# Retention's value product ahead of attention's output product, in a two-layer hybrid decoder

## The chip, the cores and the metric

The kernel runs on one core of one Trainium2 chip, in one launch. The time is the device time of one execution in microseconds (us), the median of several runs. TensorE (PE) does matrix products, VectorE (DVE) and ScalarE (ACT) do elementwise work, GpSimd (POOL) and SyncE (SP) issue DMAs here. Each engine takes its own instructions strictly in order and waits on semaphores for the others.

## The reference

There are 512 tokens of 1024 features, two layers, everything in fp32. One layer is:

```
h  = rmsnorm(x, g_mix)
aq, ak, av, rq, rk, rv, rg, ga, gb = split(h @ w_in)       # one projection
ya = sliding_window_attention(rope(aq), rope(ak), av, sinks) @ w_a
r  = retention(rot(rq), rot(rk), rv)                       # 4 heads, causal, decayed
yb = (groupnorm(r) * silu(rg)) @ w_b
x  = x + (sigmoid(ga) * ya + sigmoid(gb) * yb) @ w_out
x  = x + square(relu(rmsnorm(x, g_mlp) @ w_up)) @ w_down
```

A final rmsnorm gives the output. Attention has 8 query heads of 64 over 2 key heads, in blocks of 128 queries against a band of 256 keys, with one learned sink logit per head.

## The kernel before

**Products.** Activations lie feature by token in SBUF. Every fp32 operand is split into a high part (rounded to fp32r, by ACT: `hi`, L334) and a rest (by DVE: `lo`, L335), and one fp32 product is three PE matmuls, high x high, low x high, high x low (L386 to L388). A *unit* is 128 x 1024 of weights: 512 KB, loaded by SP into one of five buffers `raw`, split into one of four `hi` and four `lo`, used by 24 matmuls. `unit_order` writes down the order of all units once. Loads run four units ahead of splits, splits three units ahead of products. `chunk` takes one unit of `w_in` and makes 128 output features of all tokens. Units of the projection (38 in a layer) come as: a group of four (key, value, two query chunks), two query chunks, eight chunks of `ga`, rk and rq of head 0, rg 0 to 3, rk and rq of heads 1, 2, 3, rg 4 to 7, eight chunks of `gb`.

**Block products.** Retention's values `rv` (512 x 1024) and the MLP's matrices are multiplied by a scheme with seven half-size products in place of eight. `values` is that product for `rv`: 14 units (seven parts of two). It needs sums of quarters of the weights and of the activations. The sums of activations are made by `Turned`: four copies `xg` of 512 KB each are read back from DRAM (from the input `xT` in layer 0, from `spill` in layer 1), scaled by ACT (L882), added and subtracted by DVE (L885 to L888) and split (L406, L407). `load(0)` and `load(2)` issue two copies each, `build(0)` and `build(2)` do the arithmetic. The copies lie in a pool `big` of six buffers (4 KB in each partition) that they share with attention's result `whole`, with the tables and with the retention gates `z`, so a copy waits until its buffer is given back.

**Weight-sum jobs.** The sums of weights are made in DRAM: `sum_steps` is a list of jobs, each a DMA on POOL that copies a quarter (0.5 or 1 MB) and one that adds another onto it. `pace(src)` is called after the evacuation of a chunk; on every second call POOL copies one column of `src` (`mark`, which makes it wait for that evacuation) and then issues the next job.

**Attention** runs as a background generator. Its queries are rotated, split, and, for two layouts, partly copied between partitions by 16 DMAs of 64 KB on SP (`beside`, L658: `r<-qlo`); four more do the same for the keys. Then come 16 steps (4 blocks of 128 queries x 4 pairs of heads): scores on PE (`score`, L771), softmax on DVE and ACT, transposes (`pT`, L736), and per block the weighted values (`pv`, L756 and L757), whose sum `whole` is split into `a_h`, `a_l`. `advance(rate)` takes steps of it between the halves of a chunk.

**The stretch between attention and retention.** After the last step of attention stand two units (rk and rq of head 1) with `build(0)` behind them, then the four units of `w_a` (attention's output product on `a_h`, `a_l`), with `build(2)` in their middle, then `values`, at the end of which the generator `retention(0)` starts (heads 0 and 1), then rk and rq of heads 2 and 3, then rg 4 and 5.

**Clean-ups.** ACT writes some PSUM banks, and PE then adds onto them. Such a bank first gets a matmul that clears its accumulation flags: `ones` x `xh`. `values` has one for its bank of the pool `ps_aux`; in the MLP `wash` issues one or two after the first block's `w_up` chunks.

**Order.** Engines get their instructions from a scheduler that orders the program with its own estimate of times when it is built. It moves work of later program text ahead where it expects an engine to be free. The order is then fixed.

Of the kernel before, what the change touches and what calls it, by code (L numbers as in the profile page):

```python
# [17 lines left out]
P = 128  # L18
T = 512
# [31 lines left out]
DELAY = 2  # L51
AHEAD = 4
SPLIT = 3


def unit_order(layer):

    order = [("w_in", i) for i in range(4 + 2 + 8 + 2 + 4 + 2)]
    order += [("w_a", i) for i in range(4)]
    order += [("rv", part, u) for part in range(7) for u in range(2)]  # L60
    order += [("w_in", i) for i in range(22, 34)]
    order += [("w_b", i) for i in range(4)]
# [12 lines left out]
    return order  # L75
# [39 lines left out]
def decoder(ctx, tc, xT, x_first, w_in, w_rv, w_a, w_b, w_out, w_up, w_pair, w_down, w_end, tables, decay, band, g_last, out):  # L115
    nc = tc.nc
# [493 lines left out]
    def layer_body(layer):  # L610
# [48 lines left out]

        def put_k(ps):  # L660
            r = rotate(ps, attn_tabs, layer == 0)
            pace(r)
            lo = big("klo")[:, 0, :]
            for g in range(N_KV):
                nc.scalar.activation(kh[g], r, AF.Copy)
            nc.vector.tensor_tensor(lo, r, f32(kh[0]), ALU.subtract)
            for g in range(N_KV):
                nc.vector.tensor_scalar(kl[g], lo, half[:, g : g + 1], None, ALU.mult)
                beside(g, kh[g], kh[g])
# [23 lines left out]
        def put_q(c):  # L693
            def put(ps):
                r = rotate(ps, attn_tabs, layer == 0 and c < 2)
                pace(r)
                if c % 2 == 0:
                    qlo[:] = [big("qlo")]
                lo = qlo[0][:, c % 2, :]
                for g in range(N_KV):  # L700
                    nc.scalar.activation(q_s[g][:, c, :], r, AF.Copy)
                nc.vector.tensor_tensor(lo, r, f32(q_s[0][:, c, :]), ALU.subtract)
                for g in range(N_KV):
                    beside(g, q_s[g][:, c, :], lo)

            return put
# [205 lines left out]
        def values(turned, while_last):  # L912
# [7 lines left out]
            def multiply(ps, moving, start=True, meanwhile=None):  # L920
                for u in range(2):
                    hi, lo = unit("rv", layer)
                    if meanwhile:
                        meanwhile()
# [41 lines left out]
            put(0, 1, c, 1, two)  # L966
            multiply(b, turned[3], False)
            put(1, 1, b, -1, five)
            while_last()
            multiply(b, turned[4], False, advance)  # L970
            turned.free(1)
            put(1, 0, b, -1)

# [98 lines left out]
        def retention(pair):  # L1072
            two = [Head(2 * pair), Head(2 * pair + 1)]
            for head in two:
                for js in ((0, 1), (2, 3)):
                    head.scores(js)
                    if pair == 0 and head is two[1] and js[0]:
                        load_decay(1)
# [12 lines left out]
            yield  # L1091
            yield
            two[1].norm()
            yield
# [19 lines left out]
        qk(1)  # L1114
        turned.build(0)
        turned.load(2)


        aT = [(a_h[:, c, :], a_l[:, c, :]) for c in range(4)]
        for u in range(4):  # L1120
            hi, lo = unit("w_a", layer)
            for j in range(2):
                c = 2 * u + j
                ps = bank(ps_mm, "mm")
                pairs = []
                for k in range(4):
                    cols = slice(k * 256 + j * P, k * 256 + (j + 1) * P)
                    pairs.append(((hi[:, cols], lo[:, cols]), aT[k]))
                products(ps, pairs, True, True)
                nc.vector.tensor_tensor(mixed[c], mixed[c], ps, ALU.mult)  # L1130
            if u == 1:
                turned.build(2)
                load_decay(0)
        for t in a_t:
            slots.give(*t[1])

        values(turned, lambda: background.append(retention(0)))
        qk(2, 1.2)
        qk(3, 1.2)
        for i in (4, 5):  # L1140
            chunk("w_in", layer, xs, put_rg(i), 1.2)
        drain()
        background.append(retention(1))
        for i in (6, 7):
# [239 lines left out]
        def down(e, into):  # L1384
# [16 lines left out]
            a, c = ([bank(ps_mm, "mm") for _ in range(2)] for _ in range(2))  # L1401
            b = [bank(ps_aux, "b") for _ in range(2)]
            multiply(a, b11)
            for m in range(2):
                nc.scalar.activation(b[m], a[m], AF.Copy)
            multiply(c, u_forms[0])
# [166 lines left out]
        def first_hooks():  # L1573
# [11 lines left out]
                    nc.scalar.activation(sq[:, 0:1], factor[:, 0:1], AF.Sqrt)  # L1585
                sum_input(2)

            def wash():
                for ps in used:
                    nc.tensor.matmul(ps, ones, xh[:, 0, :], start=True, stop=True)  # L1590

            return at0, at1, wash

        for e in range(N_BLOCK):
            if e == 0:
                into = Adding(e)
                hooks = first_hooks()
                for c in (0, 2):
                    two_chunks("w_up", layer, xs, [put_up(c), put_up(c + 1)], hooks[c // 2])
                hooks[2]()  # L1600
# [51 lines left out]
def _w_in_units(w):  # L1652
# [11 lines left out]
    def qk(h):  # L1664
        return _units_chunks(w, pairs(O_RK, h)) + _units_chunks(w, pairs(O_RQ, h))
# [4 lines left out]
    units += qk(0)  # L1670
    units += _units_chunks(w, O_RG + r(T))
    units += qk(1)
    units += qk(2) + qk(3)
    units += _units_chunks(w, O_RG + T + r(T))
    units += _units_chunks(w, O_GB + r(D))
    return units

# [108 lines left out]
```

## Time and profile before

| | us |
|---|---|
| three runs | 1508.51, 1501.99, 1509.72 (median 1508.51) |
| the profiled execution | 1502.61, of which its span is 1500.8 |
| PE busy | 1465.7, 98% of the span |
| DVE busy | 1124.4, 75% |
| ACT busy | 949.0, 63% |
| POOL busy | 218.1, 15% |
| granted PE clock, mean | 0.99 of full speed |

PE is busy all but 35 us of the span. In the views below a wait is put down to what ended it; a time stands in us from the start of the span, layer 0 takes the first half and layer 1 the second.

### The profile page before, as it was taken

To read this page: it belongs to the slowest core of one execution; us is meant where nothing else is said; L and a number is where in the kernel's file an instruction comes from. 1 tells how busy PE (TensorE), PEld (TensorE's weight loads), DVE (VectorE), ACT (ScalarE), POOL (GpSimd) and SP (SyncE) were. 2 spreads that over 40 slices of the span, in tenths; PEclk is the share of its full clock that TensorE was granted. 3 is DMA by queue.
4 is the path that set the end of the run, shared out by engine and by line. 5 is a ranking of instruction groups with operands and counts; after the bars stand their busy time and mean duration, and the time that the engine had idled before them with its cause. 6 is when DMAs were issued, how large, how long until landed. Compare 5 with 4: busy or idle time off the path is not lost.

```text
span 1500.8 us, 21396 instructions
## 1 busy us (share of the span) xinstructions
PE 1465.7 (98%) x7753; PEld 1262.4 (84%) x7753; DVE 1124.4 (75%) x1697; ACT 949.0 (63%) x1553; POOL 218.1 (15%) x294
## 2 busy tenths in 40 slices
PE   9899999999999999999999988999999999999998
PEld 7688788888889999998877876888888889999997
DVE  6668887865577888888876687787846768888885
ACT  7546656543467777777754475565434767777775
POOL 0210000302211111112202010002120021111120
PEclk9999999999999999999999998999999999999999
DMA  7954653859875777666959646447696286776664
GB/s 256 268 174 137 200 176 105 230 135 282 234 185 189 190 197 182 181 177 196 299 166 293 198 116 188 159 127 196 180 292 187 77 214 187 197 195 173 177 187 154
DMA packets 95867, 287.32 MB, mean 191 GB/s; under 512 B 11152, under 2 KB 11280, under 8 KB 90896
## 3 DMA queue, kind: packets, MB, share of 16 engines
q1 hardware_dynamic: 62544, 175.56, 34.1%
q0 software_dynamic: 32496, 109.07, 32.8%
q8 instruction: 61, 1.00, 0.3%
q10 hardware_dynamic: 720, 1.31, 0.2%
q14 instruction: 46, 0.38, 0.1%
HBM read 246.05 MB, written 107.48 MB: 236 GB/s over the span
## 4 chain that ended last, share of the span: by engine, by line
PE 91%; DMA 4%; DVE 2%; ACT 2%; issue 1%; SPq 0%; ACTq 0%; DVEq 0%
PE mm L386 24%; PE mm L387 24%; PE mm L388 24%; PE b L386 3%; PE b L387 3%; PE b L388 3%; DMA r<-qlo 2%; PE rv L386 2%; PE rv L388 2%; PE rv L387 2%; PE mm L401 1%; DMA xg<-spill 1%; PE score L771 1%; DVE lo L335 1%; PE r L388 1%; PE r L387 1%
## 5 line engine op out<-in xcount | busy, mean ns | idle before, releaser
L334 ACT ACTIVATE hi<-raw 128x1024 fp32r<-128x1024 f32 (+1 forms) x375 | 382.4, 1020 | 319.3 <-PE mm L387 190.0
L335 DVE TENSOR_TENSOR lo<-raw,hi 128x1024 fp32r<-128x1024 f32 (+1 forms) x376 | 438.8, 1173 | 145.5 <-ACT hi L334 143.6
L386 PE MATMUL mm<-xh,hi 128*128 128x512 f32 (+1 forms) x976 | 345.4, 356 | 1.8 <-DVE z L983 1.0
L387 PE MATMUL mm<-xl,hi 128*128 128x512 f32 (+1 forms) x976 | 344.1, 355 | 0.0
L388 PE MATMUL mm<-xh,lo 128*128 128x512 f32 (+1 forms) x976 | 342.6, 356 | 0.0
L386 PE MATMUL mm<-r,hi 128*128 128x256 f32 (+1 forms) x736 | 239.7, 329 | 8.1 <-ACT r L406 7.6
L387 PE MATMUL mm<-r,hi 128*128 128x256 f32 (+1 forms) x736 | 240.0, 326 | 0.0
L388 PE MATMUL mm<-r,lo 128*128 128x256 f32 (+1 forms) x736 | 240.0, 326 | 0.0
L386 PEld LDWEIGHTS mm<-xh,hi 128*128 128x128 f32 x976 | 185.4, 190 | 26.7 <-ACT xh L409 1.2
L387 PEld LDWEIGHTS mm<-xl,hi 128*128 128x128 f32 x976 | 185.5, 190 | 24.5
L388 PEld LDWEIGHTS mm<-xh,lo 128*128 128x128 f32 x976 | 184.6, 190 | 24.6
L386 PEld LDWEIGHTS mm<-r,hi 128*128 128x128 f32 x736 | 141.3, 192 | 22.4 <-ACT r L406 8.4
L387 PEld LDWEIGHTS mm<-r,hi 128*128 128x128 f32 x736 | 140.6, 191 | 13.3
L388 PEld LDWEIGHTS mm<-r,lo 128*128 128x128 f32 x736 | 140.5, 191 | 11.8 <-DVE lo L335 0.2
L1464 POOL DMA_DIRECT2D y<-eu x56 | 62.2, 1341 | 370.6 <-DVE eu L1449 370.6
L387 PE MATMUL mm<-lo,r 128*128 128x512 f32 (+1 forms) x276 | 104.5, 388 | 0.0
L388 PE MATMUL mm<-hi,r 128*128 128x512 f32 (+1 forms) x276 | 101.4, 387 | 0.0
L386 PE MATMUL mm<-hi,r 128*128 128x512 f32 (+1 forms) x276 | 98.5, 390 | 0.4 <-ACT r L406 0.2
L386 PE MATMUL b<-hi,r 128*128 128x512 f32 x180 | 70.5, 392 | 0.0
L387 PE MATMUL b<-lo,r 128*128 128x512 f32 x180 | 70.3, 391 | 0.0
L388 PE MATMUL b<-hi,r 128*128 128x512 f32 x180 | 67.8, 390 | 0.0
L270 DVE TENSOR_TENSOR raw<-raw 128x512 f32<-128x512 f32 x56 | 38.6, 690 | 36.5 <-DMA raw<-w_pair_in 25.4
(300 smaller groups left out, 2410.6 us busy)
## 6 DMA issues: line engine op xcount, KB each, us to landing
raw<-w_in_in SPq DMA_DIRECT2D x73, 512.0 KB, 4.4
sums_down<-w_down_in POOLq DMA_DIRECT2D x30, 1024.0 KB, 10.5
sums_up<-w_pair_in POOLq DMA_DIRECT2D x56, 512.0 KB, 8.9
raw<-w_down_in SPq DMA_DIRECT2D x45, 512.0 KB, 7.2
raw<-w_pair_in SPq DMA_DIRECT2D x84, 256.0 KB, 3.8
y<-y POOLq DMA_DIRECT2D x64, 256.0 KB, 9.2
y<-eu POOLq DMA_DIRECT2D x62, 256.0 KB, 8.1
raw<-sums_down SPq DMA_DIRECT2D x30, 512.0 KB, 7.5
```

The costliest lines, as they stand in the source:

```text
L270: nc.vector.tensor_tensor(raws[i][:, at], last[:, LEFT], last[:, RIGHT], ALU.add)
L334: nc.scalar.activation(hi[:, at], raw[:, at], AF.Copy)
L335: nc.vector.tensor_tensor(lo[:, at], raw[:, at], f32(hi[:, at]), ALU.subtract)
L386: nc.tensor.matmul(ps, ah, bh, start=start and i == 0, stop=False, **more)
L387: nc.tensor.matmul(ps, ah, bl, start=False, stop=False, **more)
L388: latest[0] = nc.tensor.matmul(ps, al, bh, start=False, stop=stop and i == n - 1, **more).ins
L401: latest[0] = nc.tensor.matmul(ps, w[:, cols(j, c)], moving[k][low], start=first, stop=bool(final)).ins
L771: nc.tensor.matmul(ps[:, g * w : (g + 1) * w], q_s[g][:, c, at], part[:, keys], start=i == 0, stop=i == 1)
L1464: nc.gpsimd.dma_start(y[:, 2 * j + m, i * T : (i + 1) * T], t, **how)
```

## The change

The stretch between attention and retention is reordered. After rk and rq of head 1 now stand rg 4 and rg 5, then `values`, then the units of `w_a`; `retention(0)` starts after `w_a`, and rk and rq of heads 2 and 3 advance it at a rate of 2.0 in place of 1.2. `build(2)` and the first decay table come ahead of `values`. The host lays the weights out in the new order. `pace` is no longer called at the key and the queries (5 calls fewer in a layer), and is called at the eight chunks of `w_a`. `wash` is gone; the first blocks of the MLP clean the banks that ACT is about to write, right after the product that fills their source. The second decay table is loaded later. The line numbers of the new kernel are higher by one in its first half and lower by one to four from there on.

```diff
+CLEANED = ({1: (0,)}, {0: (0, 1), 1: (0,)})
 def unit_order(layer):
-    order = [("w_in", i) for i in range(4 + 2 + 8 + 2 + 4 + 2)]
+    order = [("w_in", i) for i in range(4 + 2 + 8 + 2 + 4 + 2 + 2)]
+    order += [("rv", part, u) for part in range(7) for u in range(2)]
     order += [("w_a", i) for i in range(4)]
-    order += [("rv", part, u) for part in range(7) for u in range(2)]
-    order += [("w_in", i) for i in range(22, 34)]
+    order += [("w_in", i) for i in range(24, 34)]
@@ put_k @@
             r = rotate(ps, attn_tabs, layer == 0)
-            pace(r)
@@ put_q @@
                 r = rotate(ps, attn_tabs, layer == 0 and c < 2)
-                pace(r)
...
         qk(1)
         turned.build(0)
         turned.load(2)
+        for i in (4, 5):
+            chunk("w_in", layer, xs, put_rg(i))
+        turned.build(2)
+        load_decay(0)
+        values(turned)
@@ the units of w_a @@
                 nc.vector.tensor_tensor(mixed[c], mixed[c], ps, ALU.mult)
-            if u == 1:
-                turned.build(2)
-                load_decay(0)
+                pace(mixed[c])
...
-        values(turned, lambda: background.append(retention(0)))
-        qk(2, 1.2)
-        qk(3, 1.2)
-        for i in (4, 5):
-            chunk("w_in", layer, xs, put_rg(i), 1.2)
+        background.append(retention(0))
+        qk(2, 2.0)
+        qk(3, 2.0)
         drain()
@@ down @@
             multiply(a, b11)
+            with tc.issue_after(latest[0]):
+                for m in CLEANED[last].get(e, ()):
+                    nc.tensor.matmul(b[m], ones, xh[:, 0, :], start=True, stop=True)
...
-            def wash():
-                for ps in used:
-                    nc.tensor.matmul(ps, ones, xh[:, 0, :], start=True, stop=True)
```

PE in layer 0, where the fourth score of attention stands (`score_639` before, `score_631` after; `mm_772` and `mm_764` are the same chunk of `ga`, `pT` a transpose of attention). Before:

```order
L386 MATMUL mm_772<-xh_76,hi_568 128x512
L387 MATMUL mm_772<-xl_77,hi_568 128x512
L771 MATMUL score_639<-r2_83,r0_81 128x128 x2
L771 MATMUL score_639<-r2_83,r1_82 128x128 x2
L736 MATMUL pT_656<-ident_130,sm_537 128x128 x2
L388 MATMUL mm_772<-xh_76,lo_569 128x512
L386 MATMUL mm_867<-xh_76,hi_634 128x512
```

After:

```order
L389 MATMUL mm_684<-xh_76,lo_509 128x512
L387 MATMUL mm_764<-xh_76,hi_557 128x512
L388 MATMUL mm_764<-xl_77,hi_557 128x512
L770 MATMUL score_631<-r2_83,r0_81 128x128 x2
L770 MATMUL score_631<-r2_83,r1_82 128x128 x2
L735 MATMUL pT_648<-ident_130,sm_530 128x128 x2
L389 MATMUL mm_764<-xh_76,lo_558 128x512
```

The score stood one matmul ahead of the end of that chunk and stands now two behind its start: 263 matmuls of chunks are ahead of it before, 242 after.

ACT in layer 0 at the end of attention (`whole` is attention's last result and `r4` its split `a_h`; `rot2` belongs to rk and rq; `xg` are the copies of `Turned`, `t2` the first sum that DVE makes from the first two). Before:

```order
L627 ACTIVATE rot2_1501<-mm_1475 64x512
L628 ACTIVATE rot2_1501<-mm_1475 64x512
L882 ACTIVATE xg_1465<-xg_1465,x_75 128x512 x2
L406 ACTIVATE r4_85<-whole_1372 128x4x128
L627 ACTIVATE rot2_1545<-mm_1519 64x512
L628 ACTIVATE rot2_1545<-mm_1519 64x512
L882 ACTIVATE xg_1466<-xg_1466,x_75 128x512 x2
```

After:

```order
L407 ACTIVATE r4_85<-whole_1364 128x4x128
L881 ACTIVATE xg_1457<-xg_1457,x_75 128x512 x2
L881 ACTIVATE xg_1458<-xg_1458,x_75 128x512 x2
L628 ACTIVATE rot2_1533<-mm_1507 64x512
L629 ACTIVATE rot2_1533<-mm_1507 64x512
L335 ACTIVATE hi_1598<-raw_1461 128x1024
L407 ACTIVATE r2_83<-rot_1492 128x512
L881 ACTIVATE xg_1560<-xg_1560,x_75 128x512 x2
L407 ACTIVATE r0_81<-t2_1549 128x512
```

The split of attention's last result stood behind the first copy's scaling and stands now ahead of it; the third copy's scaling (`xg_1560`) stands now ahead of the first split that `values` reads (`r0<-t2`).

PE in layer 0 at the start of what follows attention (`rv` are the banks of `values`, `ret` scores of retention, `mm_1578` the first bank of `w_a`). Before:

```order
L757 MATMUL pv_1380<-r7_88,r3_84 128x512
L916 MATMUL rv_1726<-xh_76,ones_115 128x512
L386 MATMUL ret_1978<-late_89 128x512
L387 MATMUL ret_1978<-late_89 128x512
L388 MATMUL ret_1978<-late_89 128x512
L386 MATMUL ret_1986<-late_89 128x384
L387 MATMUL ret_1986<-late_89 128x384
L388 MATMUL ret_1986<-late_89 128x384
L386 MATMUL mm_1578<-r4_85,hi_1421 128x512
```

After:

```order
L389 MATMUL rv_1653<-hi_1564,xl_77 128x512
L387 MATMUL ret_2102<-late_89 128x512
L388 MATMUL ret_2102<-late_89 128x512
L389 MATMUL ret_2102<-late_89 128x512
L387 MATMUL ret_2110<-late_89 128x384
L388 MATMUL ret_2110<-late_89 128x384
L389 MATMUL ret_2110<-late_89 128x384
L387 MATMUL rv_1656<-hi_1682,r0_81 128x512
```

Before, the last `pv` of attention is followed by the clean-up, six matmuls of retention and then `w_a`, which reads `a_h`. After, between that last `pv` and the first matmul that reads a sum of `Turned` (`r0`) stand 9 matmuls of rq, 48 of rg 4 and 5, the clean-up, 24 of the first part of `values` and the same six of retention in layer 0; in layer 1, where the last `pv` stands in the middle of rg 4, it is 9 of rg 4, the clean-up, 24 of rg 5, 24 of `values` and the six.

More of the change, by code (lines that the diff above doesn't have):

```diff
@@ L910, in quarter, with values @@
             return [(xh[:, k, at], xl[:, k, at]) for k in range(4 * half, 4 * half + 4)]
-        def values(turned, while_last):
+        def values(turned):
             a, c = ([bank(ps_mm, "rv") for _ in range(2)] for _ in range(2))
@@ L918, in values, with multiply @@
             nc.vector.tensor_scalar(minus, plus, -1.0, None, ALU.mult)
-            def multiply(ps, moving, start=True, meanwhile=None):
+            def multiply(ps, moving, start=True):
                 for u in range(2):
                     hi, lo = unit("rv", layer)
-                    if meanwhile:
-                        meanwhile()
                     for m in range(2):
@@ L968, in values @@
             put(1, 1, b, -1, five)
-            while_last()
-            multiply(b, turned[4], False, advance)
+            multiply(b, turned[4], False)
             turned.free(1)
@@ L1076, in retention @@
                     head.scores(js)
-                    if pair == 0 and head is two[1] and js[0]:
-                        load_decay(1)
                     yield
@@ L1093, in retention @@
             two[1].norm()
+            if pair == 0:
+                load_decay(1)
             yield
@@ L1586, in at1 @@
                 sum_input(2)
-            def wash():
-                for ps in used:
-                    nc.tensor.matmul(ps, ones, xh[:, 0, :], start=True, stop=True)
-            return at0, at1, wash
+            return at0, at1
         for e in range(N_BLOCK):
@@ L1672, in _w_in_units @@
     units += qk(1)
+    units += _units_chunks(w, O_RG + T + r(2 * P))
     units += qk(2) + qk(3)
-    units += _units_chunks(w, O_RG + T + r(T))
+    units += _units_chunks(w, O_RG + T + 2 * P + r(2 * P))
     units += _units_chunks(w, O_GB + r(D))
```

1 line of the change is left out of this document (removed).

## The prediction

> **What bounds the kernel now.** I read the page first, then the waits of PE, the instructions of PE in order of time around each long wait, and last SP, ACT and the copies there.
>
> ```profile
> span 1500.8 us, 21396 instructions
> PE 1465.7 (98%) x7753; PEld 1262.4 (84%) x7753; DVE 1124.4 (75%) x1697; ACT 949.0 (63%) x1553; POOL 218.1 (15%) x294
> ```
>
> PE is the bound: 35.1 us of the span are idle. The change takes no matmul of the reference away, so it can win idle PE time and time at a low clock, nothing else. The waits of PE (total us, times, longest):
>
> ```profile
> PE mm L386 <- ACT r L406: 7.8, 3, 6.3
> PE score L771 <- DMA r<-qlo: 7.4, 5, 5.1
> PE ret L386 <- DVE whole L759: 3.9, 2, 1.9
> PE score L771 <- DVE sm L798: 1.8, 1, 1.8
> PE pT L736 <- DVE st L789: 1.1, 1, 1.1
> PE pv L756 <- ACT r L406: 1.0, 1, 1.0
> PE mm L386 <- DVE z L983: 1.0, 1, 1.0
> PE score L771 <- DVE r L407: 0.4, 1, 0.4
> PE score L771 <- DVE st L779: 0.3, 1, 0.3
> ```
>
> Nearly all of them lie between the queries and `w_a`. In order of time:
>
> ```profile
> 75.26 0.66 PE L771 MATMUL score<-r,r 128*128 128x128 f32 x2 [5.14 <-DMA r<-qlo]
> 163.51 2.08 PE L386 MATMUL mm<-r,hi 128*128 128x512 f32 x4 [1.30 <-ACT r L406]
> 806.22 0.41 PE L771 MATMUL score<-r,r 128*128 128x128 f32 x2 [0.75 <-DMA r<-qlo]
> 908.22 2.07 PE L386 MATMUL mm<-r,hi 128*128 128x512 f32 x4 [6.30 <-ACT r L406]
> ```
>
> After a wait PE's clock (PEclk, third column from the right) is low for some 4 us:
>
> ```profile
> 75.30:79.30 4.00, 3.67 (x12) 3.03 (x13) 2.08 (x6) 1.15 (x5) 0.62 (x1) 0.51 0.69 280
> 163.50:168.00 4.50, 4.49 (x11) 3.53 (x12) 4.43 (x9) 3.62 (x6) 1.33 (x3) 0.50 1.01 189
> 809.00:813.00 4.00, 4.00 (x12) 3.24 (x13) 0.00 (x0) 0.00 (x0) 0.00 (x0) 0.59 1.01 313
> 869.00:877.00 8.00, 5.15 (x32) 3.81 (x31) 7.67 (x26) 7.13 (x20) 0.00 (x0) 1.00 0.22 66
> 908.20:912.20 4.00, 3.98 (x10) 3.17 (x11) 3.79 (x7) 3.02 (x5) 0.00 (x0) 0.51 1.02 240
> 350.00:375.00 25.00, 25.00 (x111) 20.58 (x110) 10.07 (x12) 6.67 (x9) 5.08 (x7) 1.00 1.02 303
> ```
>
> So a cluster of waits costs its idle time and then busy time x (1 - PEclk): 1.8 us at 75, 2.2 at 163, 1.6 at 809, 2.0 at 908, nothing at 869. The last row gives the pitch of matmuls at full clock: 25 / 111 = 0.225 us.
>
> **The change part by part.** *Query copies (weight-sum jobs gone from keys and queries).* Layer 0 waits for `r<-qlo` 7.4 - 0.75 = 6.65 us, and 1.8 follow in low clock: 8.4. Layer 1: 0.75 + 1.82 + 1.6 = 4.2. The copies are slow because jobs fill the queues; the window 40 to 80 us holds
>
> ```profile
> q0 software_dynamic: 1008, 6.82, 62.4%
> q1 hardware_dynamic: 1824, 4.46, 30.4%
> DMA to landing us min/median/max: 6.1/11.1/14.2
> L702 DVE TENSOR_TENSOR qlo<-rot,r x4: 682/685/689, 44.7 to 53.2; 128x512 f32<-128x512 f32 x4
> 51.45 0.69 DVE L832 TENSOR_TENSOR x<-mm,rstd 128x512 f32<-128x512 f32 x1
> 59.65 3.75 SPq L658 DMA_DIRECT2D r<-qlo  x4
> raw<-w_in_in SPq DMA_DIRECT2D x73, 512.0 KB, 4.4
> ```
>
> (q0 carries POOL's jobs; the landing row is that of `qlo`'s copies; the last row is the page's.) The last query is split at 53.2 + 0.7 = 53.9, yet its four copies go out only from 59.65: SP waits for earlier copies. The new order moves its score forward by 263 - 242 = 21 matmuls, 4.7 us: PE was there at 75.26 - 5.14 = 70.1, now at 70.1 - 4.7 - 1.15 (two shorter waits gone) = 64.2. Without jobs I let the four leave 53.9 to 56.4 and land within 4.4 (what 512 KB take at the median) to 6.1 (the fastest copy here): 60.8 to 62.5, in time. One job does remain: the first now hangs on the second chunk of `ga`, evacuated at 51.45. I keep 1.0 us for it in layer 0 and 0.8 in layer 1: **-7.4 and -3.4**. Ends: -8.4 and -4.2, or the rival below.
>
> By the Trainium skill's page "DMA: Bandwidth & Descriptors" (Queues, rings and completion order) each DMA engine takes turns between the queues by packets, so an emptied POOL queue could at best halve the 11.1 us, and a copy still stands behind SP's own weight loads. If the last copy then left at 62.9 as now, it would land at 68.5, the wait be 4.3 and the sum 1490. No run here shows SP's queue alone.
>
> *End of attention.* Waits of 0.97 (layer 0) and 1.09 + 0.97 + 0.45 + 0.32 = 2.83 (layer 1) end on small steps of DVE and ACT. Attention starts earlier and, in layer 1, its last products lie beside rg 4. Gain between 0 and 3.8; I take half: **-1.9**.
>
> *`w_a` moved back.* It waited for the split of `whole`, which ACT held behind a copy's scaling. Gone with it: 1.93 + 1.30 + 2.2 = 5.5 in layer 0 and 1.93 + 6.30 + 2.0 = 10.2 in layer 1. What is late next is the sums themselves: `values` reads them, and `w_a` (96 matmuls, 21.6 us) no longer covers their copies. The third copy waits for `whole`'s buffer, the fourth for the first copy's:
>
> ```profile
> 157.73 0.39 PE L757 MATMUL pv<-r,r 128*128 128x512 f32 x1
> 164.22 0.33 SPq L872 DMA_DIRECT2D xg<-xT_in  x1
> 171.19 1.34 ACT L882 ACTIVATE xg<-xg,x 128x512 f32<-128x512 f32 x2 [1.96 <-DMA xg<-xT_in]
> 173.90 1.04 ACT L334 ACTIVATE hi<-raw 128x1024 fp32r<-128x1024 f32 x1
> 179.39 1.34 ACT L882 ACTIVATE xg<-xg,x 128x512 f32<-128x512 f32 x2 [4.45 <-DMA xg<-xT_in]
> 182.69 0.63 ACT L406 ACTIVATE r<-t 128x512 fp32r<-128x512 f32 x1 [1.01 <-DVE t L886]
> 908.92 0.32 SPq L872 DMA_DIRECT2D xg<-spill  x1
> 916.22 1.34 ACT L882 ACTIVATE xg<-xg,x 128x512 f32<-128x512 f32 x2 [2.14 <-DMA xg<-spill]
> ```
>
> From the last `pv` to the third copy's issue: 6.5 us, of which the scaling in front (1.3) goes and a `hi` split (1.04) comes: 6.2. From that issue to the split of the fourth copy's first sum: 183.3 - 164.2 = 19.1. ACT's new order puts a `hi` and an `r` split, then two `hi` and two 0.6 us sigmoids into it (5 us, of which 1.3 covers DVE's sums): 22.7. Ready at 28.9 after the last `pv`. Layer 0 has in front of it 9 + 48 + 1 + 24 matmuls, retention's six (1.4), and 26 on the first two copies: 108 x 0.225 + 1.4 + 0.2 = 26.0. Wait: 2.9. In layer 1 only 58 matmuls (14.7 us) stand before the first sum, whose split lies behind the third copy's scaling: 6.2 + 7.3 + 1.3 + 1.04 + 3 x 0.6 = 17.7, wait 3.0. Then rg 4's bank, which `values` wants 12 matmuls later (at 20.4), is evacuated only into the second copy's buffer: 17.7 + 0.6 + 1.04 + 0.6 + 1.04 + 1.2 + 0.7 = 22.9, wait 2.5. The fourth copy is hidden there by 1.5. Each layer also pays 1.9 of low clock: new cost 4.8 and 7.4. Net **-0.7 and -2.8**. Ends: no new wait at all, or both copies slow (rivals).
>
> By "TensorE: Matmul & The Clock Gate" (The HAM clock gate) of the Trainium skill the clock falls only after about 3.4 us of idling; then these short waits would cost no clock and the sum be 1482.8. The row at 809 disagrees: waits of 0.75 and 1.82 us were enough.
>
> *The rest.* Retention at rate 2.0 puts its DVE work (some 22 us) beside four chunks in place of six. DVE was full there already while PE never waited:
>
> ```profile
> 1000.00:1025.00 25.00, 25.00 (x114) 20.81 (x113) 25.00 (x34) 14.40 (x22) 4.64 (x6) 1.00 0.69 174
> 1203.22 0.50 PE L1590 MATMUL ssq<-xh,ones 128*128 128x512 f32 x1 [0.25 <-ACT y L1241]
> ```
>
> I cost it at nothing; without that cover it would be some 5 us a layer. The eight new `pace` calls send four jobs (on POOL) beside `w_a`, whose loads on SP are four units ahead; the row at 350 shows DMA queues full (1.02) with PE unbroken. Clean-ups: one matmul more, +0.2, less a wait of 0.25, plus whatever queueing them costs: **+0.2**.
>
> Sum: -7.4 - 3.4 - 1.9 - 0.7 - 2.8 + 0.2 = -16.0. The profiled execution took 1502.61: **1486.6 us**. It is near the fastest of the three runs; from the median (1508.51) the same steps lead to 1492.5. A measurement tells about 0.5% from no change: 1495.1 and 1510.1 on this scale.
>
> **The rivals.** *The sums' copies in series (slower).* The first copies of layer 1 took far longer than the later ones, with jobs around them (landing rows of the copies, 150 to 175 us and 885 to 912 us):
>
> ```profile
> DMA to landing us min/median/max: 4.8/5.5/6.9
> DMA to landing us min/median/max: 7.2/13.1/15.5
> ```
>
> In the new order copies three and four run beside loads of `rv` units and jobs. At 13.1 each, layer 0 loses 5.9 + 7.5 more, layer 1 5.8 + 8.3 - 1.5: 26.0, in all 1512.6. It eats the gain from about 11 us a copy. Against it: 5.5 to 7.3 us for these two in both layers.
>
> *Copies of queries as late as now (no change).* If they still land at 75.2, PE waits there with 21 matmuls fewer done: +4.7 for -7.4, and 0 for -3.4 in layer 1: 1502.1. For it: the first job still goes out ahead of the last copies.
>
> *All new waits covered.* If the copies land a few us earlier and ACT keeps up: -16.0 - 4.8 - 7.4, 1474.4.
>
> **How the numbers follow.** Forecast 0.58 (own range 1478 to 1497), slow copies 0.13, late queries 0.12, all covered 0.17. The range 1473 to 1503 leaves out the slow copies. Faster: 0.54 of the forecast and all covered, 0.71; within 0.5%: 0.04 + 0.12 = 0.16; slower: 0.13.
>
> **What would show it.** Right: no PE wait on `r<-qlo` over 1 us, no `mm` of `w_a` waiting for ACT, new waits of `rv` matmuls on ACT's `r` or DVE, 2 to 6 us a layer, and a wait of ACT on `xg` ahead of them. Wrong: `rv` waits above 8 us a layer, a PE wait on `score` above 4 us, or PE waiting for `lo` splits in the chunks after `w_a`.

## The result, and the profile after

| | median us | runs | ratio to before | 95% interval |
|---|---|---|---|---|
| before | 1505.90 | 1501.99 to 1509.72 (7) | 1 | |
| after | 1494.09 | 1490.09 to 1499.14 (7) | 0.9925 | 0.9900 to 0.9949 |

The change makes the kernel 0.75% faster: 1494.1 us, inside the forecast range, 7.5 us above the forecast. The profiled execution of after took 1498.12 us, one of its longer ones, 4.5 us less than that of before.

From the page of after, its span and busy times:

```profile
span 1496.4 us, 21384 instructions
PE 1464.2 (98%) x7754; PEld 1260.4 (84%) x7754; DVE 1125.0 (75%) x1697; ACT 943.1 (63%) x1549; POOL 217.4 (15%) x294
```

PE is idle for 32.2 us, 2.9 less than before. The waits of PE (total us, times, longest; those at the start, at the end and in the MLP are left out, all but one):

```profile
PE rv L387 <- ACT hi L335: 6.3, 2, 4.8
PE rv L387 <- ACT r L407: 5.9, 2, 4.5
PE rv L387 <- ACT rv L954: 5.7, 1, 5.7
PE rv L389 <- DVE r L408: 1.2, 1, 1.2
PE mm L387 <- DVE z L979: 1.0, 1, 1.0
PE rv L388 <- DVE lo L336: 0.5, 1, 0.5
PE b L1403 <- ACT y L1238: 0.2, 1, 0.2
PE mm L387 <- ACT r L407: 0.2, 1, 0.2
```

No `score` is in the list any more, and the long wait of `w_a` for ACT's `r` is down to 0.2. In their place stand waits of `rv`, that is of `values`. In order of time in layer 0, and the first one of layer 1:

```profile
171.41 1.27 PE L387 MATMUL rv<-hi,r 128*128 128x512 f32 x2 [5.69 <-ACT rv L954]
183.91 1.22 PE L387 MATMUL rv<-hi,xh 128*128 128x512 f32 x2 [4.78 <-ACT hi L335]
912.81 0.80 PE L387 MATMUL rv<-hi,r 128*128 128x512 f32 x1 [4.53 <-ACT r L407]
```

The stretches of time (PE busy first, PEclk third from the right) show the attention's start without a gap in layer 0 (800 to 825 us, in layer 1, is the same: PE busy 25.00, clock 1.00), and the low clock behind the new waits:

```profile
50.00:75.00 25.00, 25.00 (x130) 21.19 (x129) 20.01 (x69) 14.96 (x44) 3.83 (x5) 1.00 0.82 235
171.40:176.00 4.60, 4.54 (x11) 3.19 (x12) 3.61 (x5) 0.43 (x1) 0.58 (x2) 0.60 1.01 170
184.00:189.00 5.00, 5.00 (x12) 3.95 (x13) 5.00 (x8) 2.79 (x4) 0.00 (x0) 0.53 0.15 25
912.80:918.00 5.20, 4.01 (x9) 2.73 (x10) 5.20 (x8) 3.18 (x4) 1.01 (x2) 0.50 0.76 147
918.00:925.00 7.00, 6.85 (x28) 5.31 (x27) 5.74 (x7) 2.48 (x4) 1.54 (x3) 0.91 1.02 298
```

So `values` costs 5.69 + 4.78 idle and 4.54 x 0.40 + 5.00 x 0.47 in low clock, 14.6 us, in layer 0; and 9.1 (five waits) + 4.01 x 0.50 + 6.85 x 0.09, 11.7 us, in layer 1. ACT and SP of after show what is behind it in layer 0. The rows of the four copies in order of time, their scaling on ACT and their issue on SP:

```profile
153.14 1.34 ACT L881 ACTIVATE xg<-xg,x 128x512 f32<-128x512 f32 x2 [1.45 <-DMA xg<-xT_in]
157.87 1.34 ACT L881 ACTIVATE xg<-xg,x 128x512 f32<-128x512 f32 x2 [3.39 <-DMA xg<-xT_in]
165.14 1.34 ACT L881 ACTIVATE xg<-xg,x 128x512 f32<-128x512 f32 x2 [3.11 <-DMA xg<-xT_in]
170.78 1.05 ACT L954 ACTIVATE rv<-rv 128x512 f32<-128x512 f32 x2
179.59 1.33 ACT L881 ACTIVATE xg<-xg,x 128x512 f32<-128x512 f32 x2 [7.76 <-DMA xg<-xT_in]
140.02 13.40 SPq L871 DMA_DIRECT2D xg<-xT_in  x3
170.43 0.33 SPq L871 DMA_DIRECT2D xg<-xT_in  x1
```

And the time from issue to landing of the first three:

```profile
DMA to landing us min/median/max: 12.0/13.1/17.2
```

ACT waits for a copy four times. Behind the third copy's scaling (with splits in between) stands the bank copy (`rv`, L954) for which PE waits 5.69 us, behind the fourth's the split (`hi`) for which it waits 4.78. ACT's own waits for these two copies are 3.11 and 7.76. The first three copies took 12.0 to 17.2 us, where before's four took 4.8 to 6.9 in this layer.

POOL of after at that time shows the weight-sum jobs (`mark` is the copy that a job hangs on; `sums_up`, `sums_down` are the job's two DMAs):

```profile
137.53 0.64 POOL L247 COPY mark<-late 128x1 f32<-128x1 f32 x1 [44.80 <-ACT late L407]
138.11 0.54 POOL L223 DMA_DIRECT2D sums_up<-w_pair_in  x1
...
139.18 1.06 POOL L247 COPY mark<-z 128x1 f32<-128x1 f32 x1
139.59 1.09 POOL L223 DMA_DIRECT2D sums_down<-w_down_in  x1
...
145.22 0.18 POOL L247 COPY mark<-z 128x1 f32<-128x1 f32 x1 [0.46 <-DVE z L979]
145.67 0.53 POOL L223 DMA_DIRECT2D sums_up<-w_pair_in  x1 [0.26 <-issue]
```

POOL stands 44.8 us at a mark on `late` (the split of head 0's rq). Behind it the mark on `z` (rg 1) does not wait at all: its chunk had been evacuated already. The job of rg 3 goes out soon after, when its own chunk is evacuated. Three jobs go out within 8 us, and the copies are issued from 140.0, into the middle of them. The copies have moved as well: before issues its first two at 154.9, some 10 us behind its second job (144.3) and ahead of its third (159.6).

### The profile page after: what moved, and what is told of

It is laid out like the page before. It is cut to its first block, busy times and chain, and to the rows that moved or that the text cites. A ratio compares the mean times of both kernels' runs of the same rounds, so it can differ in the third digit from the quotient of the medians.

```text
span 1496.4 us, 21384 instructions
## 1 busy us (share of the span) xinstructions
PE 1464.2 (98%) x7754; PEld 1260.4 (84%) x7754; DVE 1125.0 (75%) x1697; ACT 943.1 (63%) x1549; POOL 217.4 (15%) x294
## 4 chain that ended last, share of the span: by engine, by line
PE 92%; DMA 3%; ACT 2%; DVE 1%; issue 1%; ACTq 0%
PE mm L387 24%; PE mm L388 24%; PE mm L389 24%; PE b L387 3%; PE b L388 3%; PE b L389 3%; DMA xg<-xT_in 2%; PE rv L387 1%; PE rv L388 1%; PE rv L389 1%; PE mm L402 1%; PE score L770 1%; PE pT L735 1%; PE r L388 1%; DMA xg<-spill 1%; PE r L389 1%
```

## The experiments

The theory that these traces suggest: the gain comes from the jobs gone from the queries, and the reorder gives part of it back because the copies for `values` land late. The rivals: the gain is the reorder's; or the copies are late because of buffers and ACT's order, not because of traffic. Eleven kernels ran, each timed beside the kernel before.

| run | us | ratio, 95% interval | PE idle (span - busy) |
|---|---|---|---|
| old order, jobs moved | 1502.73 | 0.9956 to 0.9978 | 38.0 |
| new order, jobs at queries | 1512.08 | 1.0024 to 1.0054 | 41.0 |
| new order, no jobs near copies | 1481.82 | 0.9815 to 0.9845 | 20.6 |
| third order | 1496.70 | 0.9915 to 0.9941 | 30.0 |
| new order, one call more | 1486.02 | 0.9837 to 0.9875 | 22.1 |
| old order, four calls less | 1488.06 | 0.9854 to 0.9896 | 24.0 |
| old order, no jobs near copies | 1482.55 | 0.9819 to 0.9853 | 18.9 |
| third order, no jobs near copies | 1469.33 | 0.9734 to 0.9769 | 11.6 |
| third order, one call more | 1487.21 | 0.9834 to 0.9881 | 22.4 |
| third order, quiet, jobs at queries | 1490.64 | 0.9864 to 0.9903 | 26.4 |
| new order, no call at head 0 | 1483.48 | 0.9816 to 0.9849 | 19.3 |

### The two halves of the change

Old order with the jobs moved (on before):

```diff
             r = rotate(ps, attn_tabs, layer == 0)
-            pace(r)
...
                 r = rotate(ps, attn_tabs, layer == 0 and c < 2)
-                pace(r)
...
                 nc.vector.tensor_tensor(mixed[c], mixed[c], ps, ALU.mult)
+                pace(mixed[c])
```

> The kernel before, with one part of the change alone: no weight-sum jobs at the key and the queries, and jobs at the chunks of `w_a` instead; the order of the units, `wash` and everything else stay as before. Theory A (the gain is the jobs gone from the queries; the reorder by itself costs time, because the copies for `values` land late): the waits on `score` go (7.4 us of idle and 3.4 us at a low clock by before's trace, 12.6 us with what attention's own steps lose less), the two clusters of waits of `w_a` stay (5.5 and 10.2 us), and the time is 1505.9 - 12.6, about 1493, as fast as the kernel after or faster. Rival B (the reorder brings the gain, the jobs' place does not matter): 1506, within 4 us of before, with a wait on `score` above 4 us.

Measured 1502.73, 4.3 us under before. No wait of `score` for `r<-qlo` was left, as theory A said, but the gain fell short by 10 us. PE in this run:

```profile
191.69 0.76 PE L386 MATMUL rv<-hi,r 128*128 128x512 f32 x1 [5.61 <-DVE x L1128]
907.26 2.08 PE L386 MATMUL mm<-r,hi 128*128 128x512 f32 x4 [8.33 <-ACT r L406]
```

And the landing of layer 0's four copies, 4.8 to 6.9 us before:

```profile
DMA to landing us min/median/max: 10.5/15.6/19.8
```

Slow copies come with the jobs' part of the change, in the old order too. Neither theory had that.

New order with the jobs back at key and queries and none at `w_a` (on after):

```diff
             r = rotate(ps, attn_tabs, layer == 0)
+            pace(r)
...
                 r = rotate(ps, attn_tabs, layer == 0 and c < 2)
+                pace(r)
...
-                pace(mixed[c])
```

> The kernel after, with the weight-sum jobs put back at the key and the queries and taken from the chunks of `w_a`: the reorder and the queued clean-ups without the jobs' part. Theory A: PE waits on `score` again, and by more than before since 21 matmuls fewer stand ahead of it in layer 0; the time is 1494.1 + 12.6 + about 4, so 1507 to 1511, no faster than before. Rival B: about 1494, with no wait on `score` above 2 us.

Measured 1512.08, slower than before by 0.24% to 0.54%: a little above theory A. PE waited 9.8 us on `r<-qlo`. Theory A's reason for a longer wait does not hold: with the jobs back at the queries the fourth score stands behind 263 matmuls of chunks, as in the kernel before, and layer 0 waits 6.5 us, as before (6.6). It is layer 1 that waits longer, 3.3 us in place of 0.75.

The two halves do not add. Alone, the jobs' part gives 4.3 us and the reorder with the clean-ups costs 5.0; together they give 11.8. Beside the jobs' part the reorder is worth some 8 us (1502.73 to 1494.09), so it does not give part of the gain back, as the theory had it: the slow copies cost the old order more. What it is worth depends on where the jobs fall.

### Traffic, or buffers and ACT's order

No jobs near the copies (on after; the calls taken away are made up for at every second chunk of `w_a` and `gb`):

```diff
-                pace(f32(view(hi)))
+                if h != 1:
+                    pace(f32(view(hi)))
...
-                pace(rg[i])
+                if i > 5:
+                    pace(rg[i])
...
                 pace(mixed[c])
+                if j:
+                    pace(mixed[c])
...
-            chunk("w_in", layer, xs, gate(gates[c]))
+            chunk("w_in", layer, xs, gate(gates[c], c % 2))
```

> The kernel after, with no weight-sum jobs between rq and rk of head 1 and rg 5 (8 calls fewer), so that none is in flight while the four copies `xg` are read; the same 4 jobs are issued at `w_a` and at the chunks of `gb`. In the trace of after these copies took 9.1 to 17.2 us from issue to landing in layer 0 and 4.1 to 10.2 in layer 1, and PE waited 10.5 and 9.1 us in `values`. Theory C (the jobs' traffic makes the copies slow): the copies land in 4 to 7 us, the waits in `values` fall below 4 us a layer, and the time is 1494.1 - 12 to 18, so 1476 to 1482. Rival D (the copies wait for buffers that are given back late, and ACT takes the scaling in a bad order; traffic is a side matter): landings may shorten, but the waits in `values` keep at least 7 us a layer, and the time stays above 1488.

Measured 1481.82, 12.3 us under after: theory C. The waits of `values` are 3.0 us in layer 0 and 5.3 in layer 1 (4 had been expected at most), without a low clock behind them. The copies of layer 1 land in 3.8 to 4.6 us. In layer 0 one job still goes out at 140.1, 2 us ahead of the first two copies, and these take 9.6 and 10.0; the third and fourth, for which `values` waits, take 3.7.

### Why the jobs sat there: an odd number of calls

Every second call of `pace` issues a job. The change takes five calls away ahead of the copies, so each job behind them hangs on the neighbouring chunk. One call more (on after):

```diff
             r = rotate(ps, attn_tabs, layer == 0)
+            if layer == 0:
+                pace(r)
```

> The kernel after, with `pace` called once more in the whole program, at the key of layer 0. Every second call issues a job, and the change took away an odd number of calls ahead of the copies, so the jobs now hang on the other chunks. In layer 0 of before, jobs go out at 138.6, 144.3 and 159.6 us; of after, at 138.1, 139.6 and 145.7, and the copies `xg` are issued from 140.0. One more call puts them back on the old chunks in layer 0, and on the other ones in layer 1 as well. Theory P (the copies are slow because this shift heaps three jobs on them): in layer 0 the first two copies land in 5 to 8 us, the waits in `values` fall from 10.5 us to 5 or less there, with no low clock behind them, and the time is 1494.1 - 7 to 12, so 1482 to 1487. Rival Q (any job in that stretch costs as much, whichever chunk it hangs on): within 3 us of after, 1491 to 1497.

Measured 1486.02, 8.1 us under after: theory P. POOL in this run:

```profile
123.14 0.70 POOL L247 COPY mark<-late 128x1 f32<-128x1 f32 x1 [33.55 <-ACT late L407]
132.35 0.19 POOL L247 COPY mark<-z 128x1 f32<-128x1 f32 x1 [7.18 <-DVE z L981]
151.75 0.19 POOL L247 COPY mark<-z 128x1 f32<-128x1 f32 x1 [17.55 <-DVE z L981]
```

The landing of layer 0's four copies:

```profile
DMA to landing us min/median/max: 4.1/4.4/5.4
```

The mark stands now on the first of the two `late` splits and is over 14 us sooner, the other two wait for their own chunks, and no job is issued while the first two copies are under way (issued from 142.6). From 85 to 180 us as many jobs go out as in after; only their times differ. The waits of `values` in layer 0 fall from 10.5 to 3.5 us. A low clock did follow the longest of them, which theory P had excluded (below).

The same in the old order (on before):

```diff
             r = rotate(ps, attn_tabs, layer == 0)
-            pace(r)
+            if layer == 0:
+                pace(r)
...
                 r = rotate(ps, attn_tabs, layer == 0 and c < 2)
-                pace(r)
...
-            chunk("w_in", layer, xs, gate(gates[c]))
+            chunk("w_in", layer, xs, gate(gates[c], c < 3))
```

> The kernel before, without `pace` at the four queries of both layers and at the key of layer 1, and with three calls more at the chunks of `gb`: the query jobs are gone in the old order, and the jobs around the copies hang on the same chunks as before in layer 0. Theory P: layer 0 keeps before's copies (4.8 to 6.9 us) and its waits of `w_a` (3.2 us), the waits on `score` go, and the time is 1507.1 - 12.6, about 1494.5, 8 us less than with the calls taken away without regard to the shift (1502.7). Rival Q: 1500 to 1504 again, with copies of 10 us or more in layer 0.

Measured 1488.06: 18.3 us under before, 6 better than theory P, and 14.7 under the run with the calls taken away without regard to the shift. Layer 0's copies land in 3.6 to 8.4 us. In layer 1, where before has its heap, they still take 4.7 to 15.9, and `w_a` waits 5.98 us. This is the old order with no jobs at the queries, and it gives more than the whole change gives. The new order with one call more (1486.02) is not clear of it by the two intervals.

The shift has two sides: which chunk a job hangs on, and what POOL's order holds behind a mark. To tell them apart, two calls (an even number) go at rk and rq of head 0 (on after):

```diff
-                pace(f32(view(hi)))
+                if h:
+                    pace(f32(view(hi)))
```

> The kernel after, without the two `pace` calls at rk and rq of head 0, and nothing else. The number of calls ahead of the copies stays even against after, so the jobs of the chunks behind hang on the same chunks; what goes is the mark on `late`, for which POOL stood 44.8 us and behind which two more jobs were held until 139. Theory H (the heap comes from POOL's fixed order: one mark that waits for a late split holds the jobs behind it, and they go out together with the copies): the job of rg 1 goes out when its chunk is evacuated, before 137 us, the first two copies of layer 0 land in 4 to 9 us in place of 12.0 and more, and the time is 1494.1 - 5 to 11, so 1483 to 1489. Rival Q (it is the mere presence of jobs at rg 1, rg 3 and rq of head 1): within 3 us of after, 1491 to 1497.

Measured 1483.48, 10.6 us under after: theory H. POOL in this run:

```profile
133.38 0.51 POOL L247 COPY mark<-z 128x1 f32<-128x1 f32 x1 [38.49 <-DVE z L980]
146.85 0.18 POOL L247 COPY mark<-z 128x1 f32<-128x1 f32 x1 [11.55 <-DVE z L980]
```

The landing of layer 0's first three copies:

```profile
DMA to landing us min/median/max: 3.6/4.7/6.1
```

The jobs of rg 1 and rg 3 hang on the same chunks as in after. Without the mark on `late` ahead of it the first goes out 6 us sooner, 13 us apart from the second, and the copies, issued from 142.4, are fast. So jobs on rg 1 and rg 3 do not slow the copies by being there. But the edit takes the job on `late` away with its mark: two jobs stand where three stood, so this run does not tell the hold from the one job less. That the spacing is enough, with the number of jobs kept, is what the run with one call more shows.

### What the reorder is worth without the traffic

Old order, no jobs at key and queries nor from rg 0 to the end of `values` (on before; the calls are made up for at rk and rq of heads 2 and 3 and at all chunks of `gb`):

```diff
             r = rotate(ps, attn_tabs, layer == 0)
-            pace(r)
...
                 r = rotate(ps, attn_tabs, layer == 0 and c < 2)
-                pace(r)
...
-                pace(f32(view(hi)))
+                for _ in range((1, 0, 2, 2)[h]):
+                    pace(f32(view(hi)))
...
-                pace(rg[i])
+                if i > 3:
+                    pace(rg[i])
...
-            chunk("w_in", layer, xs, gate(gates[c]))
+            chunk("w_in", layer, xs, gate(gates[c], True))
```

> The kernel before, with no jobs at key and queries, and none from rg 0 to the end of `values`; they are issued at rk and rq of heads 2 and 3, at rg 4 to 7 and, doubled, at the chunks of `gb`. It is the old order with the same quiet as in the run without jobs near the copies (1481.8), so the difference of the two is what the reorder is worth when traffic is out of the way. Theory A (the reorder removes waits of `w_a` that come from ACT's order and not from traffic): `w_a` still waits 3 us in layer 0 and 3 us or more in layer 1, each with a low clock behind it, and the time is 1486 to 1491. Rival E (only the traffic matters, the order of the units does not): 1482, within 3 us.

Measured 1482.55, against 1481.82 in the new order, with intervals that overlap nearly whole: the time is rival E's. PE does wait at `w_a` and at the retention scores just ahead of it, as theory A said, 2.5 us in layer 0 and 3.7 in layer 1, with some 2 us of low clock behind the last; but the new order's waits of `values`, 3.0 and 5.3 us, cost as much. The orders trade one wait for another of the same size. The waits of the old order in layer 1, for attention's last result:

```profile
884.43 0.50 PE L386 MATMUL ret<-late 128*128 128x512 f32 x1 [1.93 <-DVE whole L757]
887.67 2.07 PE L386 MATMUL mm<-r,hi 128*128 128x512 f32 x4 [1.72 <-ACT r L406]
```

### A third order

Four units stand ahead of `w_a`, and `w_a` ahead of `values` (on after):

```diff
     order = [("w_in", i) for i in range(4 + 2 + 8 + 2 + 4 + 2 + 2)]
-    order += [("rv", part, u) for part in range(7) for u in range(2)]
     order += [("w_a", i) for i in range(4)]
+    order += [("rv", part, u) for part in range(7) for u in range(2)]
...
-        turned.build(2)
-        load_decay(0)
-        values(turned)
...
                 pace(mixed[c])
+            if u == 1:
+                turned.build(2)
+                load_decay(0)
...
+        values(turned)
         background.append(retention(0))
```

> A third order: rq and rk of head 1, rg 4, rg 5, then the units of `w_a` with `build(2)` in their middle, then `values`; no weight-sum jobs at key and queries, as in the kernel after. Both products that wait have work ahead of them: four units ahead of `w_a`, and `w_a` (21.6 us) ahead of `values`. Theory A (what is lost after the change is the cover of the copies): no wait of `w_a` on ACT above 1 us, waits in `values` below 3 us a layer, and of the 14.6 and 11.7 us that the waits of `values` cost after the change 20 or more come back: 1470 to 1476. Rival D (the chain on ACT and the buffers set the time at which the sums are ready, wherever `values` stands): `values` still waits 5 us or more in a layer, 1484 or more.

Measured 1496.70, no better than after, though both products had work ahead of them. Theory A fell. DVE and PE of this run in layer 1:

```profile
909.12 0.69 DVE L884 TENSOR_TENSOR xg<-xg 128x512 f32<-128x512 f32 x1 [12.28 <-ACT xg L881]
915.08 0.68 DVE L1126 TENSOR_TENSOR x<-x,mm 128x512 f32<-128x512 f32 x1
915.82 0.79 PE L387 MATMUL mm<-r,hi 128*128 128x512 f32 x1 [9.56 <-DVE x L1126]
```

DVE waits 12.3 us in `build(2)` for the scaling of a copy, which waits for the copy; behind it stands the evacuation of `w_a`'s bank, and PE waits for that. The copies took 5.3 to 20.6 us. With the jobs kept away as in the run of the old order above (and none at `w_a`):

> The third order (rq and rk of head 1, rg 4 and 5, the units of `w_a` with `build(2)` in their middle, then `values`), with the jobs kept away from rg 0 to the end of `values` as in the run before it. In the run of this order with jobs, `w_a` waited 4.5 and 9.6 us for DVE's evacuation of its banks, which stood behind `build(2)`'s sums, and those for the slow copies. Theory C (traffic is the cause of that too): no wait of `w_a` or `values` above 1.5 us, and of the 8.3 us of waits that the run with `values` ahead of `w_a` and without jobs keeps, 6 or more go: 1472 to 1477. Rival D (the copies' buffers come back late in this order, whatever the traffic): a wait of `w_a` of 3 us or more in a layer, 1482 or more.

Measured 1469.33, 2.3% to 2.7% under before, the best of all. In the stretches from 150 to 200 and from 900 to 950 us PE is busy throughout at a clock of 1.00; the copies land in 3.6 to 7.4 us. With the traffic gone, this order is worth 12.5 us over the new one.

Is the one call enough in this order, with all its jobs in place?

```diff
             r = rotate(ps, attn_tabs, layer == 0)
+            if layer == 0:
+                pace(r)
```

> The third order (rk and rq of head 1, rg 4 and 5, `w_a`, `values`) with all its weight-sum jobs, and `pace` called once more at the key of layer 0. It tells whether the best run (1469.3) needs the jobs taken away from the copies, or only their release on the right chunks. Theory P (the shift is all): the waits of `w_a` (4.5 and 9.6 us in this order with jobs) fall below 1.5 us, and the time is 1470 to 1476. Rival R (the four jobs at the chunks of `w_a` meet copies three and four in this order, whatever the shift): these copies take 10 us or more, `w_a` or `values` waits 3 us or more in a layer, 1479 to 1490.

Measured 1487.21: the time of rival R, but for the most part not at its place. The copies land at a median of 5.6 us in layer 0 and 6.7 in layer 1, one of layer 0 takes 12.6, and `w_a` waits 2.7 us once. More is lost behind it: 3.4 us of waits around 225 us and 3.3 around 959. POOL's marks there and a PE wait that follows, in order of time:

```profile
179.49 0.18 POOL L247 COPY mark<-z 128x1 f32<-128x1 f32 x1 [9.11 <-DVE z L981]
181.04 0.46 POOL L247 COPY mark<-x 128x1 f32<-128x1 f32 x1
224.73 0.50 PE L387 MATMUL mm<-xh,hi 128*128 128x512 f32 x1 [2.55 <-ACT hi L335]
```

The loads of `w_in` units issued on SP from 200 to 225 us (KB each, median us to landing):

```profile
raw<-w_in_in SPq DMA_DIRECT2D x5, 512.0 KB, 10.2
```

A mark on `z` (rg 5) holds the marks of `w_a` (on `x`) in POOL's order; those wait for nothing when their turn comes, so their jobs go out in a heap as well. The DMA engines are full from 190 to 220 us (busy share 1.03 to 1.04; 0.35 to 0.65 in the quiet run, that without jobs near the copies), and the next weight loads take 10.2 us in place of 4.0 in the quiet run. PE then waits for a split of such a unit, and its clock is 0.59 from 224.7 to 233.0. No run spreads these jobs, so that it is the heap, and not the jobs at `w_a` as such, is argued and not shown.

Last, the query jobs alone, put back into the best run:

```diff
             r = rotate(ps, attn_tabs, layer == 0)
+            pace(r)
...
                 r = rotate(ps, attn_tabs, layer == 0 and c < 2)
+                pace(r)
```

> The best run so far (third order, no jobs near the copies, 1469.3) with `pace` put back at the key and the queries, and nothing else: the query term by itself, with no other wait of the stretch in the way. By the trace of before, that term is 8.4 us in layer 0, 4.2 in layer 1 and up to 3.8 at the end of attention. Theory A (these add up): waits on `score` come back, and the time is 1469.3 + 12.6 to 16.4, 1482 to 1486. Rival F (what attention loses at its start is given back, since the work behind it has slack in this order): below 1477. Rival G (the 21 matmuls fewer ahead of the score in layer 0 add to the wait): 1487 or more.

Measured 1490.64, 21.3 us above the best run: the time of rival G, but not its reason. From the waits list of PE:

```profile
PE score L772 <- DMA r<-qlo: 11.4, 5, 4.9
```

Layer 0 has 6.7 us of it, as the kernel before, and its score stands behind 263 matmuls, as there: the 21 come back with the jobs. Layer 1 has 4.7, where before has 0.75. Idle time is 14.8 us more and the mean clock 0.995 in place of 0.999, which is some 6 us.

## Why the prediction was right, and where its step failed

**Bound.** PE stayed the bound in every run (97 to 99% busy), and the differences are idle PE time and low clock for the most part, as the prediction took it.

**Query copies: right, sized too low.** The wait on `r<-qlo` is gone whole in both layers (8.4 and 4.2 us; the prediction held back 1.0 and 0.8 for a job that cost nothing). The copies' landing row, in the view that gave before's 11.1, is for after:

```profile
DMA to landing us min/median/max: 1.9/2.5/7.4
```

The estimate after the Trainium skill's page "DMA: Bandwidth & Descriptors" (Queues, rings and completion order), that an emptied queue halves this at best and leaves a wait of 4.3, is not borne out: it fell to less than a quarter, and nothing waits. The measurement decides. The prediction put the score's 21 matmuls down to the new order; by the traces they go with the jobs. The old order without jobs at the queries has the score some 20 matmuls earlier too, and the new order with them has it behind 263. Alone, the jobs at the queries cost 18.3 us in the old order (where later jobs moved as well) and 21.3 in the third, against the 12.6 of the trace of before.

**End of attention: right.** Of the 3.8 us, 2.8 went (a wait of 0.98 on `z` is left); the forecast was half.

**`w_a` moved back: the mechanism right, its size wrong.** The old waits are gone, and the new ones stand where the prediction put them: on the bank copy behind the third copy's scaling, on a split behind the fourth's, on ACT's `r`. But they cost 14.6 and 11.7 us where 4.8 and 7.4 had been forecast, so the term is +9.1 and +1.5 in place of -0.7 and -2.8. By the prediction's own sign of being wrong, waits of `rv` above 8 us a layer, this term failed: they are 10.5 and 9.1 us. The step that failed is the landing of the copies: it was taken over from before, where the third and fourth took 6.9 and 5.5 us in layer 0, 7.2 and 4.7 in layer 1. After, they took 12.0 and 9.1 in layer 0, and 10.2 and 6.8 in layer 1, and layer 0's first two 13 us and more. Where the copies of layer 0 are fast again, in the run with one call more, `values` waits 3.5 us in layer 0 and 5.3 in layer 1; 2.9 and 5.5 had been forecast. The reason was in reach: the prediction had seen that the first job now hangs on the second chunk of `ga`, and used this at the queries only. In layer 0 the same shift puts a job on rq of head 0, whose split is late, and the job of rg 1 is held behind it. In layer 1 the calls come out even again, and after keeps the heap that before has there. Before's rows, where its first copies were slow:

```profile
886.65 0.65 POOL L246 COPY mark<-late 128x1 f32<-128x1 f32 x1 [49.78 <-ACT late L406]
888.33 0.48 POOL L246 COPY mark<-z 128x1 f32<-128x1 f32 x1
```

**The sum.** In the two traces: -8.4 - 4.2 - 2.8 + 9.1 + 1.5 = -4.8, measured -4.5. The forecast was -16.0. The medians differ by 11.8: the profiled execution of before was one of its shorter and that of after one of its longer, and what the other executions of the two kernels did differently no trace shows. So that the time lies in the range is luck in part. The `w_a` terms were out by 14.1 us in all, of which the query and attention terms gave back 2.7; the rest was covered by the width of the range and by the 7 us between the traced pair and the medians. With the jobs put off the copies by one call, the new order takes 1486.0.

**Rivals.** The copies in series came half true (four copies between 9.1 and 17.2 us in layer 0, two of 10.2 and 6.8 in layer 1), the late query copies not at all. (In that rival's sum the 5.9 should be 6.2, by the 6.9 us of the third copy; its 1512.6 hardly moves.) That all new waits are covered, 1474.4, was within reach of this order only without the traffic (1481.8).

**Low clock.** Behind the waits of 5.69, 4.78 and 4.53 us PE ran 4 to 5 us at about half clock, which cost 1.8, 2.35 and 2.0; the prediction had 1.9 a layer, for one such place in each.

**The rest.** No wait appears where retention runs at rate 2.0, and the queued clean-ups leave a wait of 0.2 us in place of 0.25. No run changes either alone, so their share is read from the trace, not shown.

## What to carry to other kernels

Where background transfers hang on marks in an in-order queue, follow the queue row by row: a mark on a result that comes late holds the jobs behind it, and they go out close together and slow whatever latency-bound copy meets them. Removing an odd number of calls of an every-second-time pacer moves all later jobs, so look at the places far behind the edit too. A reorder that trades one wait for another shows its own worth only when the traffic is out of the way: here nothing for the order that was tried, and 12.5 us for a third one. Beside traffic the same reorder cost 5.0 us or gave some 8, by where the jobs fell, so the halves of such a change are not to be added up.

## What was not expected of the hardware

Waits of the same size lowered the clock in one place and not in another. In the run with one call more, a wait of 2.44 us was followed by a clock of 0.50 (172 to 176 us), while waits of 2.32 and 1.58 us, 3.7 us apart, left it at 1.00. The same wait of the same matmul, 35 us behind the wait before it, stands also in the run with no call at head 0. That run first, then the one with one call more and its clock (third from the right):

```profile
901.12 0.69 PE L389 MATMUL rv<-hi,r 128*128 128x512 f32 x1 [2.31 <-DVE r L408]
906.75 0.50 PE L389 MATMUL rv<-hi,r 128*128 128x512 f32 x1 [2.32 <-DVE r L408]
906.70:910.40 3.70, 2.11 (x8) 1.42 (x8) 3.67 (x5) 0.62 (x2) 0.00 (x0) 1.00 0.46 131
```

Behind the 2.31 us the clock is 0.57 (901 to 905), behind the 2.32 it is 1.00: the length of the wait does not decide. The Trainium skill's "TensorE: Matmul & The Clock Gate" (The HAM clock gate) has the activity judged in free-running windows of some 3.4 us. That a shorter wait counts or not by where it falls agrees with these rows; no trace here shows the windows.

Small copies suffered much from the jobs: 64 KB landed in 2.5 us (median) without jobs at the queries and in 11.1 with them. And the quieter kernels vary less: 1480.64 to 1482.00 without jobs near the copies, 1490.09 to 1499.14 for after.
